# Adaptive-norm modulation blocks as fp32 column-group products in a two-layer hybrid backbone

## The chip, the cores and the metric

One NeuronCore of one Trainium2 chip runs the whole program in one launch. The metric is the device time of a run in microseconds (us). The engines are PE (TensorE: matmuls, with its weight loads shown apart as PEld), DVE (VectorE), ACT (ScalarE), POOL (GpSimd) and SP (SyncE, which here only issues transfers). They run side by side, and each works through its own instructions in order.

## The reference

Two layers work on 256 latent and 256 context tokens of width 1024. Each layer is a SwiGLU feed-forward (FFN) half-step, a token mixer, and a second FFN half-step. Every sub-layer is modulated by columns that come from one product per layer, of a conditioning vector with a 1024 x 9216 matrix:

```python
m_lat = (silu(c) @ w_ada[l] + b_ada[l])       # 9 * 1024 columns, for the latent tokens
m_ctx = silu(c_ctx) @ w_ada[l] + b_ada[l]     # the same matrix, for the context tokens

def modulate(xs, m, j):
    return xs * (1 + m[3 * j + 1]) + m[3 * j]

def ffn_sublayer(xs, m, j, wg, wu, wd, g, b):
    y = 0.5 * swiglu(modulate(xs, m, j), wg, wu, wd)
    return layer_norm(ALPHA * xs + m[3 * j + 2] * y, g, b)
```

## The kernel before, in words

Activations lie transposed: 8 chunks of 128 features (`k` or `j`) by 512 token columns (context first, then latent). Each fp32 operand of a large product is split into a high and a low part (`whi`/`wlo` for a weight, `hH`/`hL` for the modulated input, `aH`/`aL` for the FFN's inner activations), and PE runs three products of the parts (line 420, 256 columns each). ACT makes the high part by a cast (line 282), DVE or POOL the low part by a subtraction (`split_lo`, line 620).

The order of all loads is one list, `seq` (lines 169 to 205): "x" is an input piece, "w" a weight unit of 512 KB, and the rest are pieces of `w_ada`. A block `b` is 512 of the 9216 columns; it comes in four pieces `kp` of 512 KB, each with two of the eight `k`. SP issues the loads in the order of `seq`. Weights and most pieces share five buffers ("raw"); `use_one` (line 271) consumes the next item, and a buffer comes free when its last reader is done. The pieces of blocks 1 and 3 go to the six buffers of another pool (`own_room`).

The modulation blocks are computed in three ways:

- Blocks 0 to 3 of layer 0 ("s" items, lines 291 to 297) hold shift and scale of the first FFN. Each piece is split like a weight on ACT and on DVE or POOL, and `sum_parts` (line 1286) multiplies the parts on PE with the four-column `scol2`; the 4 x 512 rows are copied (`direct_rows`), turned into columns by four transposes (`direct_cols`) and added to the bias (`direct_bias`).
- Most later blocks ("a" items, lines 298 to 322) are summed on DVE: for each `k` and token stream one multiply-add of 128 x 512 (lines 317 and 319), the last one written as halves into a `fold` tile (line 313). `red_step` (line 367), called after each FFN step, then takes the block through four ages: POOL adds the two halves (line 381), ACT and POOL split the sum (lines 385 and 386), PE sums over partitions with `pick` and ACT copies the rows (lines 359 and 364), PE transposes them (line 350) and DVE adds the bias (line 343).
- One block of layer 1 ("p" items, lines 323 to 336) is multiplied directly in fp32, `scol` (two columns) against the raw piece, in the pause of the last mixer's layer norm (`norm_latent`, line 647; `run_direct`, line 410).

At the start (lines 1343 to 1402) PE transposes the inputs (`stream_chunk`), the blocks 0 and 2 give the modulation of chunks 0 to 3, `first_input(j)` (line 1320) builds `hH` and `hL` of chunk j, and `go([j])` (line 439) runs the first four gate and up units (tiles `gu`) over chunk j: 24 products. Blocks 1 and 3 do the same for chunks 4 to 7. `in_turn` (line 1403) later subtracts the token mean, which comes from `xs`, a sum of the chunks on POOL (line 1399), by one PE product (line 1405).

The FFN (`ffn`, line 758) then goes through its gate and up units in steps `m` of 96 products, with the "a" items of layer 0 interleaved, and through the down products (tiles `dn`).

## Time and profile before

| | us |
|---|---|
| median of 3 runs (lowest, highest) | 1822.42 (1820.31, 1823.8) |
| the profiled execution's own time | 1820.95 |
| its span on the core | 1819.2 |

The profile is one execution. Its span is the time from the core's first to its last recorded instruction; the execution's own time is 1.75 us longer, and 1.47 us below the median of the runs. A busy engine is one with an instruction in flight; a matmul's record contains the end of its pipeline, so records of successive matmuls overlap and a steady stream is read from starts per time.

### The profile page before, as it was taken

To read this page: it belongs to the slowest core of one execution; us is meant where nothing else is said; L and a number is where in the kernel's file an instruction comes from. 1 tells how busy PE (TensorE), PEld (TensorE's weight loads), DVE (VectorE), ACT (ScalarE), POOL (GpSimd) and SP (SyncE) were. 2 spreads that over 40 slices of the span, in tenths; PEclk is the share of its full clock that TensorE was granted. 3 is DMA by queue.
4 is the path that set the end of the run, shared out by engine and by line. 5 is a ranking of instruction groups with operands and counts; after the bars stand their busy time and mean duration, and the time that the engine had idled before them with its cause. 6 is when DMAs were issued, how large, how long until landed. Compare 5 with 4: busy or idle time off the path is not lost.

```text
span 1819.2 us, 33814 instructions
## 1 busy us (share of the span) xinstructions
PE 1729.1 (95%) x14145; PEld 1658.0 (91%) x14145; DVE 1282.1 (70%) x1857; ACT 742.0 (41%) x1191; POOL 460.2 (25%) x326
## 2 busy tenths in 40 slices
PE   6899999999899999999999999999999989989997
PEld 4789999998798899999999989999999878879997
DVE  6899799956685678866565568865653768676565
ACT  4322232233757545422222364223223466655443
POOL 3435133243542044110101140100000466150000
PEclk8999999999999999999999999999999999999999
DMA  8367555643213225644454326665563232357662
GB/s 292 98 187 204 151 171 169 185 126 93 71 47 93 70 71 147 185 140 143 127 172 120 90 59 185 178 183 159 179 184 95 82 105 70 105 158 214 183 198 83
DMA packets 375080, 253.32 MB, mean 139 GB/s; under 512 B 8144, under 2 KB 336336, under 8 KB 374928
## 3 DMA queue, kind: packets, MB, share of 16 engines
q1 hardware_dynamic: 373856, 248.81, 46.4%
q8 instruction: 111, 1.82, 0.4%
q0 software_dynamic: 1072, 2.36, 0.4%
q14 instruction: 41, 0.34, 0.1%
HBM read 250.09 MB, written 1.05 MB: 138 GB/s over the span
## 4 chain that ended last, share of the span: by engine, by line
PE 74%; DVE 17%; ACT 5%; issue 2%; DMA 1%; POOL 0%; SPq 0%; DVEq 0%; ACTq 0%
PE gu L420 39%; PE dn L420 21%; PE head L420 5%; DVE acc L319 3%; PE pj L420 3%; PE wo L420 2%; DVE wlo L620 1%; DVE ri L939 1%; DVE h L1324 1%; PE o L1133 1%; DVE aL L620 1%; DVE xl L906 1%; ACT whi L282 1%; DVE xT L754 1%; PE adap L359 1%
## 5 line engine op out<-in xcount | busy, mean ns | idle before, releaser
L420 PE MATMUL gu<-hH,whi 128*128 128x256 f32 x2336 | 493.8, 281 | 8.3 <-ACT hH L1326 6.8
L420 PE MATMUL gu<-hH,wlo 128*128 128x256 f32 x2336 | 492.2, 280 | 6.8 <-DVE wlo L620 6.4
L420 PE MATMUL gu<-hL,whi 128*128 128x256 f32 x2336 | 492.2, 280 | 1.7 <-POOL hL L620 0.9
L282 ACT CAST whi<-raw 128x1024 fp32r<-128x1024 f32 (+1 forms) x319 | 318.8, 1025 | 177.6 <-PE dn L420 70.8
L420 PEld LDWEIGHTS gu<-hH,whi 128*128 128x128 f32 x2336 | 372.0, 190 | 13.0 <-ACT hH L1326 7.3
L420 PEld LDWEIGHTS gu<-hH,wlo 128*128 128x128 f32 x2336 | 371.9, 190 | 7.8 <-DVE wlo L620 7.2
L620 DVE TENSOR_TENSOR wlo<-raw,whi 128x1024 fp32r<-128x1024 f32 (+2 forms) x250 | 313.2, 1256 | 88.0 <-ACT whi L282 79.9
L420 PEld LDWEIGHTS gu<-hL,whi 128*128 128x128 f32 x2336 | 370.7, 190 | 2.5 <-DVE hL L620 1.4
L620 POOL TENSOR_TENSOR wlo<-raw,whi 128x1024 fp32r<-128x1024 f32 (+2 forms) x110 | 217.0, 1979 | 440.2 <-ACT whi L282 414.8
L319 DVE SCALAR_TENSOR_TENSOR acc<-raw,scol,acc 128x512 f32<-128x512 f32 x337 | 291.4, 912 | 1.0
L420 PE MATMUL dn<-aH,whi 128*128 128x256 f32 x1280 | 285.0, 282 | 6.0 <-DVE xT L754 2.9
L420 PE MATMUL dn<-aL,whi 128*128 128x256 f32 x1280 | 280.7, 279 | 0.3 <-DVE aL L620 0.3
L420 PE MATMUL dn<-aH,wlo 128*128 128x256 f32 x1280 | 280.8, 279 | 0.0
L420 PEld LDWEIGHTS dn<-aH,whi 128*128 128x128 f32 x1280 | 208.4, 189 | 11.1 <-DVE xT L754 4.5
L420 PEld LDWEIGHTS dn<-aH,wlo 128*128 128x128 f32 x1280 | 208.0, 189 | 0.2
L420 PEld LDWEIGHTS dn<-aL,whi 128*128 128x128 f32 x1280 | 207.4, 188 | 0.7 <-DVE aL L620 0.7
L767 ACT CAST aH<-pr 128x512 fp32r<-128x512 f32 (+1 forms) x88 | 50.0, 568 | 369.0 <-DVE pr L766 369.0
L766 DVE TENSOR_TENSOR pr<-sg,gu 128x512 f32<-128x512 f32 (+1 forms) x84 | 51.6, 614 | 166.0 <-PE gu L420 111.1
L754 DVE SCALAR_TENSOR_TENSOR xT<-dn,gate,xT 128x256 f32<-128x256 f32 x174 | 78.0, 478 | 83.5 <-PE dn L420 83.0
L381 POOL TENSOR_TENSOR fold<-fold 128x512 f32<-128x512 f32 x24 | 49.3, 2054 | 267.1 <-DVE fold L313 267.1
L420 PE MATMUL pj<-hH,whi 128*128 128x256 f32 x384 | 84.7, 289 | 5.3 <-ACT pt L1102 2.8
L364 ACT COPY rows<-adap 2x512 f32<-2x512 f32 x31 | 17.5, 575 | 162.2 <-PE adap L359 162.2
(267 smaller groups left out, 2377.4 us busy)
## 6 DMA issues: line engine op xcount, KB each, us to landing
raw<-in_w_ada_dram SPq DMA_DIRECT2D x136, 512.0 KB, 4.6
raw<-in_ff_gate_dram SPq DMA_DIRECT2D x88, 512.0 KB, 4.1
raw<-in_ff_up_dram SPq DMA_DIRECT2D x88, 512.0 KB, 4.7
raw<-in_ff_down_dram SPq DMA_DIRECT2D x64, 448.0 KB, 4.0
raw<-in_w_in_dram SPq DMA_DIRECT2D x36, 512.0 KB, 3.9
raw<-in_ff_down_dram SPq DMA_DIRECT2D x32, 512.0 KB, 4.4
raw<-in_w_out_dram SPq DMA_DIRECT2D x16, 512.0 KB, 3.6
in<-in_w_ada_dram SPq DMA_DIRECT2D x8, 512.0 KB, 6.7
```

Source lines behind the costliest of these rows:

```text
L282: S.copy(h_[:, :n], t[:, :n])
L319: V.scalar_tensor_tensor(out=a[:, st], in0=t[:, kk * 512:(kk + 1) * 512], scalar=sc_, in1=a[:, st], op0=ALU.mult, op1=ALU.add)
L359: PE.matmul(pp[0:2, :], lhsT=pick[:, n - 1], rhs=parts[:, i], start=(i == 0), stop=(i == 1))
L381: G.tensor_tensor(out=a[:, 0], in0=a[:, 0], in1=a[:, 1], op=ALU.add)
L420: PE.matmul(o[:, c], lhsT=w, rhs=X[:, k, c], start=first and i == 0, stop=last and i == len(halves) - 1)
L620: (eng or V).tensor_tensor(out=dst_l, in0=src, in1=dst_h.bitcast(F32), op=ALU.subtract)
L754: V.scalar_tensor_tensor(out=xT[:, j, a:b], in0=ps[:, a:b], scalar=gate[:, st, j:j + 1], in1=xT[:, j, a:b], op0=ALU.mult, op1=ALU.add)
L766: V.tensor_tensor(out=pr[:, c], in0=sg[:, c], in1=up[:, c], op=ALU.mult)
L767: S.copy(aH[:, m, c], pr[:, c])
L906: V.scalar_tensor_tensor(out=t3[:, :, off:], in0=s3[:, :, :256 - off], scalar=w[tp], in1=t3[:, :, off:], op0=ALU.mult, op1=ALU.add)
L939: V.reciprocal(gates[c, d][0], gates[c, d][0])
L1133: PE.matmul(o[c][r, a:b], lhsT=vk[c][:, x_ * 128 + 64 * p_:x_ * 128 + 64 * p_ + 64], rhs=pt[c, p_, h][:, kc * 256:(kc + 1) * 256], start=( ...
```

## The change

Blocks 0 to 3 of layer 0 become "p" items: no split, but the raw piece is multiplied in fp32. The stationary operand is `scol_z`, 32 columns per `k` of which two are `scol` and 30 zero; it lies in the tile `AB`, which the mixer overwrites, so `padded_scol` writes it at the start and again in `run_direct`. Product `k` writes the 32 PSUM partitions of column group `k % 4`. `to_cols` multiplies the copied 128 x 512 result with `join`, which adds the four groups while it turns rows into columns. The token mean comes from eight fp32 products on PE between blocks 0 and 2, in place of POOL's sum. Later blocks lose two ages: DVE adds the halves, and `to_cols` with an fp32 `pick` takes the place of split, sum, copy and transposes. `first_input` writes `hH` from `xT` on ACT. In `norm_streams` the reductions of the last two blocks are gone, since `red_step` no longer keeps any.

```diff
-    pick = const.tile([128, 2, 2], F32R, name="pick")
+    pick = const.tile([128, 2, 2], F32, name="pick")
+    join = const.tile([128, 2], F32, name="join")
+    scol_z = AB[:, 0].rearrange("p a (k s) -> p (a k) s", s=32)
...
-    seq = [("x", i) for i in range(4)] + [("s", 0, b, kp) for b in (0, 2) for kp in range(4)]
-    seq += [("w", u) for u in range(4)] + [("s", 0, b, kp) for b in (1, 3) for kp in range(4)]
+    seq = [("x", i) for i in range(4)] + [("p", 0, b, kp) for b in (0, 2) for kp in range(4)]
+    seq += [("w", u) for u in range(4)] + [("p", 0, b, kp) for b in (1, 3) for kp in range(4)]
...
-        elif it[0] == "s":
-            h_, l_ = part_tiles(*it[2:])
-            n = 512 if it[2] > 1 and it[3] == 3 else 1024
-            for a in range(0, 1024, n):
-                S.copy(h_[:, a:a + n], t[:, a:a + n])
-                split_lo(l_[:, a:a + n], t[:, a:a + n], h_[:, a:a + n], eng)
-            parts.append((it, h_, l_))
...
-                PE.matmul(acc[l, b][0:2, :], lhsT=scol[:, k, :], rhs=t[:, kk * 512:(kk + 1) * 512],
-                          start=(k == 0), stop=(k == KD - 1))
+                PE.matmul(acc[l, b][32 * (k % 4):32 * (k % 4) + 32, :], lhsT=scol_z[:, k, :],
+                          rhs=t[:, kk * 512:(kk + 1) * 512], start=(k < 4), stop=(k >= 4))
...
+    def to_cols(a, w, pool=None):
+        tp = (pool or mps)("adat")
+        for q in range(4):
+            PE.matmul(tp[:, q * 2:q * 2 + 2], lhsT=a[:, q * 128:(q + 1) * 128], rhs=w, start=True, stop=True)
+        return tp
+
+    def direct_rows(l, b):
+        r = s512("rows")
+        S.copy(r, acc.pop((l, b)))
+        return r
...
             if age == 1:
                 a = acc.pop((l, b))
-                if needs_ctx(l, b):
-                    G.tensor_tensor(out=a[:, 0], in0=a[:, 0], in1=a[:, 1], op=ALU.add)
+                if n == 2:
+                    V.tensor_tensor(out=a[:, 0], in0=a[:, 0], in1=a[:, 1], op=ALU.add)
                 r[3] = a[:, 0]
             elif age == 2:
-                part = acc_p.tile([128, 2, 512], F32R, tag="acc", name="part")
-                S.copy(part[:, 0], r[3])
-                split_lo(part[:, 1], r[3], part[:, 0], G)
-                r[3] = part
-            elif age == 3:
-                if len(pend_red) <= keep:
-                    continue
-                red_sum(r)
-                red_rows(r)
-            elif age == 4:
-                ada_finish(l, b, r[3])
+                ada_bias(l, b, to_cols(r[3], pick[:, n - 1]), 2)
                 pend_red.remove(r)
...
+    def padded_scol():
+        G.memset(scol_z, 0.0)
+        V.tensor_copy(scol_z[:, :, 0:2], scol)
+
     def run_direct():
+        padded_scol()
         while seq[ptr["use"]][0] == "p":
             use_one()
...
-            S.copy(hH[:, j], h32)
+                by = [mod[:, i, st, j:j + 1] for i in range(2)]
+                S.activation(out=hH[:, j, a:b], in_=xT[:, j, a:b], func=AF.Identity, scale=by[0], bias=by[1])
...
+        use(4)
+        rows = [direct_rows(0, 0)]
+        mp = mps("mean")
+        for j in range(KD):
+            PE.matmul(mp, lhsT=onesD, rhs=xT[:, j], start=(j == 0), stop=(j == KD - 1))
+        mean = s512("xmean")
+        S.activation(out=mean, in_=mp, func=AF.Copy, scale=ALPHA)
+        use(4)
+        direct_bias(0, rows[0])
+        rows.append(direct_rows(0, 2))
+        direct_bias(2, rows[1])
+        for j in range(4):
+            use(1)
+            first_input(j)
         tl = [gps("gu") for _ in range(4)]
         go = proj_start(list(range(4)), tl, (hH, hL), True)
-        go([0], 0, 512)
...
+        for j in range(4):
+            go([j], 0, 512)
+            use((0, 2, 2, 4)[j])
+        rows = [direct_rows(0, b) for b in (1, 3)]
+        for b, r in zip((1, 3), rows):
+            direct_bias(b, r)
-        xs = s512("xs")
-        for j in range(1, KD):
-            G.tensor_tensor(out=xs, in0=xs if j > 1 else xT[:, 0], in1=xT[:, j], op=ALU.add)
         for j in range(4, 8):
             first_input(j)
```

On PE, between the input transposes and the first `gu` products (`adap` are the modulation products, `adat` the turning of rows into columns, `mean` the token mean), before:

```order
L1333 MATMUL xtp<-cs,in 128x128 x32
L1293 MATMUL adap<-whi,scol_146 4x512 x2
L1293 MATMUL adap<-wlo,scol_146 4x512 x2
...
L1310 MATMUL adat<-cs,rows 128x4 x4
L1293 MATMUL adap<-whi,scol_146 4x512 x2
L1293 MATMUL adap<-wlo,scol_146 4x512 x2
L1310 MATMUL adat<-cs,rows 128x4 x4
L420 MATMUL gu<-hH,whi 128x256 x2
```

and in the change:

```order
L1271 MATMUL xtp<-cs,in 128x128 x32
L315 MATMUL adap<-raw,AB 32x512 x8
L1288 MATMUL mean<-xT,onesD 128x512 x8
L315 MATMUL adap<-raw,AB 32x512 x8
L332 MATMUL adat<-join,rows 128x2 x8
L391 MATMUL gu<-hH,whi 128x256 x2
```

Thirty-two products on split parts became sixteen on the raw pieces, with the eight mean products between the two blocks and both turnings behind the second block.

On DVE, at the same place (`h` is the modulated chunk in fp32, `hL` its low part, `wlo` the low part of a weight), the change has:

```order
L1275 COPY xT<-xtp 128x512 x4
L1254 TENSOR_TENSOR mod<-adat,add_152 128x2x4 x2
L591 TENSOR_TENSOR wlo<-raw,whi 128x1024
L1263 TENSOR_SCALAR h_286<-xT,mod 128x256 x2
L591 TENSOR_TENSOR hL<-h_286,hH 128x512
L591 TENSOR_TENSOR wlo<-raw,whi 128x1024
L1263 TENSOR_SCALAR h_298<-xT,mod 128x256 x2
```

The splits of the `w_ada` pieces are gone from it, and the low parts of the four weights, two of them POOL's before, now alternate with the chunks.

On PE, in the layer norm of the last mixer (`wo` is the output projection's last product, `m` the norm's sums), before:

```order
L420 MATMUL wo<-aL,whi 128x256
L329 MATMUL adap<-raw,scol 2x512 x2
L497 MATMUL m_17990<-s_17782,onesD 128x256
L497 MATMUL m_17991<-s_17783,onesD 128x256
L329 MATMUL adap<-raw,scol 2x512 x6
L420 MATMUL gu<-hH,whi 128x256
```

and on DVE in the change, where the copy into `AB` stands behind the norm's last step (`L494` and `L497` normalise chunk 0):

```order
L490 TENSOR_TENSOR m_17658<-y,m_17658 128x256
L494 TENSOR_TENSOR xT<-xT,y 128x256
L378 COPY AB<-scol 128x8x2
L497 TENSOR_TENSOR xT<-xT,m_17658 128x256
```

PE keeps its order there, but the six products now read `AB`, and so come after this copy.

## Rows read from the trace of the kernel before

**Rows 1.** The page, part 1: busy time, share of the span, instructions by engine.

```profile
PE 1729.1 (95%) x14145; PEld 1658.0 (91%) x14145; DVE 1282.1 (70%) x1857; ACT 742.0 (41%) x1191; POOL 460.2 (25%) x326
```

**Rows 2.** Windows: stretch, length, busy us (matmuls started) per engine, granted clock, DMA.

```profile
80.00:180.00 100.00, 90.97 (x744) 88.62 (x743) 97.23 (x117) 29.07 (x40) 42.67 (x27) 0.97 0.60 180
240.00:260.00 20.00, 20.00 (x179) 20.00 (x178) 19.58 (x29) 6.16 (x8) 8.28 (x4) 1.00 0.53 155
280.00:320.00 40.00, 38.23 (x317) 36.23 (x316) 39.69 (x58) 11.84 (x16) 16.34 (x8) 1.00 0.62 184
```

**Rows 3.** Waits of PE from 72 to 190 us: total, times, longest.

```profile
PE gu L420 <- DVE wlo L620: 5.9, 3, 2.5
PE dn L420 <- ACT aH L767: 2.8, 1, 2.8
```

**Rows 4.** Timeline of PE at the start: start us, length us, instruction, [idle before <- releaser].

```profile
10.20 6.06 PE L1333 MATMUL xtp<-cs,in 128*128 128x128 f32 x29 [0.78 <-DMA in<-in_x_dram]
...
32.17 0.80 PE L420 MATMUL gu<-hH,whi 128*128 128x256 f32 x2 [4.08 <-ACT hH L1326]
...
61.57 0.50 PE L420 MATMUL gu<-hH,whi 128*128 128x256 f32 x2 [0.99 <-ACT hH L1326]
...
75.00 1.02 PE L1405 MATMUL mean<-xs,onesD 128*128 128x512 f32 x2
```

**Rows 5.** The page, part 6: loads, KB each, median us from issue to landing.

```profile
raw<-in_ff_gate_dram SPq DMA_DIRECT2D x88, 512.0 KB, 4.1
```

**Rows 6.** Timeline of DVE, at the start and in the FFN.

```profile
26.90 1.23 DVE L620 TENSOR_TENSOR wlo<-raw,whi 128x1024 fp32r<-128x1024 f32 x1 [0.70 <-ACT whi L282]
...
28.70 2.77 DVE L1324 TENSOR_SCALAR h<-xT,mod 128x256 f32<-128x256 f32 x2
...
65.88 0.69 DVE L620 TENSOR_TENSOR hL<-h,hH 128x512 fp32r<-128x512 f32 x1 [0.69 <-ACT hH L1326]
66.49 0.74 DVE L1324 TENSOR_SCALAR h<-xT,mod 128x256 f32<-128x256 f32 x2
...
129.63 2.73 DVE L319 SCALAR_TENSOR_TENSOR acc<-raw,scol,acc 128x512 f32<-128x512 f32 x4
```

**Rows 7.** Timeline of ACT: a copy of rows, and a high part straight from `xT`.

```profile
24.36 0.57 ACT L1304 COPY rows<-adap 4x512 f32<-4x512 f32 x1
...
1620.78 0.60 ACT L634 ACTIVATE hH<-xT,mod 128x256 fp32r<-128x256 f32 x1 [0.87 <-DVE xT L526]
```

**Rows 8.** Timeline of PE in the first mixer: turnings, and products on two column halves.

```profile
560.82 0.60 PE L1092 MATMUL vtp<-cs,vt 128*128 128x128 f32 x4
...
561.82 2.81 PE L1133 MATMUL o<-pt,vtok 128*64 128x256 f32 x24
```

**Rows 9.** Groups by line, PE, whole run: count | busy us, mean ns | idle before.

```profile
L359 PE MATMUL adap<-part,pick 128*2 128x512 f32 x62 | 19.2, 399 | 0.0
...
L350 PE MATMUL adat<-cs,rows 2*128 2x2 f32 x128 | 12.5, 201 | 0.0
```

**Rows 10.** Groups by line, POOL, 72 to 190 us.

```profile
L620 POOL TENSOR_TENSOR wlo<-raw,whi 128x1024 fp32r<-128x1024 f32 x10 | 28.3, 2827 | 69.2 <-ACT whi L282 69.2
L381 POOL TENSOR_TENSOR fold<-fold 128x512 f32<-128x512 f32 x4 | 6.8, 1694 | 3.6 <-DVE fold L313 3.6
L620 POOL TENSOR_TENSOR part<-fold,part 128x512 fp32r<-128x512 f32 x4 | 6.3, 1567 | 0.4 <-ACT part L385 0.4
```

**Rows 11.** Groups by line, DVE, 72 to 190 us.

```profile
L319 DVE SCALAR_TENSOR_TENSOR acc<-raw,scol,acc 128x512 f32<-128x512 f32 x60 | 62.1, 1091 | 0.0
L620 DVE TENSOR_TENSOR wlo<-raw,whi 128x1024 fp32r<-128x1024 f32 x10 | 14.4, 1438 | 0.3 <-ACT whi L282 0.3
```

**Rows 12.** Timeline of PE in the last mixer's layer norm.

```profile
1609.68 3.55 PE L329 MATMUL adap<-raw,scol 128*2 128x512 f32 x4 [2.05 <-DVE xT L754]
...
1614.63 5.31 PE L329 MATMUL adap<-raw,scol 128*2 128x512 f32 x12
1621.43 0.38 PE L420 MATMUL gu<-hH,whi 128*128 128x256 f32 x1 [1.49 <-ACT hH L634]
```

More of the change, by code (lines that the diff above doesn't have):

```diff
@@ L211 @@
     acc = {}
-    parts = []
     pend_red = []
@@ L700, in norm_streams @@
         advance(head[2], G)
-        for r in pend_red:
-            assert r[2] == 3
-            red_sum(r, gps)
+        assert not pend_red
         for i, _ in enumerate(nm.newton(cc)):
@@ L825, in ffn @@
                 proj([u], [t], (aH, aL), c0, c1)
-                red_step(2 if last and nxt else 0)
+                red_step()
                 add_gated(j, t, gate, sts)
@@ L1403, in in_turn @@
         def in_turn():
-            mp = mps("mean")
-            PE.matmul(mp, lhsT=onesD, rhs=xs, start=True, stop=True)
-            mean = s512("xmean")
-            S.activation(out=mean, in_=mp, func=AF.Copy, scale=ALPHA)
-            yield
             for j in range(KD):
```

141 lines of the change are left out of this document (21 added, 120 removed).

## The prediction

> **What bounds the kernel now.** I read the busy shares first: PE is busy 95% of the span, so the time is PE's work plus the places where PE starves [rows 1]. Then the windows, to find those places. Well fed, PE starts 179 products in 20 us, 0.112 us each [rows 2]. From 80 to 180 us it starts 744 where 895 would fit; the 151 missing are worth 16.9 us. DVE is busy 97 of these 100 us, and the granted clock is 0.97: part of the stretch ran at the lower of its two levels, 1.2 instead of 2.4 GHz, which comes after PE's pauses. From 280 to 320 us the same is seen in small: 317 of 358, 4.6 us [rows 2]. The waits name the releasers, low weight parts and high parts of activations, both due behind DVE's queue, 8.7 us in all [rows 3]. Last I followed the first 76 us in order of time. The input transposes end at 16.3 us. The first gate product starts at 32.2, the products of chunk 4 at 61.6, and the first step's last product is followed by the mean, over at about 75.9 with two records of 0.43 us [rows 4]. This first step holds 192 products, 21 us of work; the rest of its 43 us is waiting for modulation blocks and for DVE.
>
> So the change touches a bound in two places: the start, where everything waits for blocks 0 to 3, and the stretch up to 180 us, where DVE sets the pace.
>
> **Prices.** One fp32 product over 512 columns shows as two records, which start 0.43 us apart, 0.855 in all (the mean: 1.02 minus the last record's 0.59 is 0.43) [rows 4]. What four column groups make of it no row shows. The nearest are the mixer's products on two halves of the columns: 24 records over 256 columns in 2.81 us, 0.11 us each after the tail, where one such record alone would take 0.214 [rows 8]. The two halves ran side by side in full. The lower bound is four side by side, 0.214 us per product of 512 columns; the upper bound is none, 0.855. I take 0.214, since the row is at its own full factor.
> The Trainium skill states another rule ("TensorE: Matmul & The Clock Gate", Part 3, The mechanism): matmuls start and end in strict program order, whatever their place in the array. This case's two-group row does not decide it for four groups. It is the second case below.
>
> **The start, part by part.** Removed are 16 splits (each 1.05 us on ACT and 1.2 on DVE or 2.4 on POOL), 64 short products (0.31 us of busy time each by the nearest form [rows 9]) and POOL's seven sums. Added are 32 fp32 products, eight for the mean, and the copies of 128 rows, which I price as the copies of four rows were, 0.57 us [rows 7], ACT's time going by columns.
>
> - The transposes end at 16.3 as now; four pieces have landed by then or soon after. Block 0: 8 x 0.214 = 1.7, to 18.0. The mean: 8 x 0.855 = 6.8, to 24.8; it stands ahead of block 2, so block 2 pays for it although its pieces, issued as block 0 frees the buffers and 4.1 us in flight [rows 5], land by 23. Block 2: to 26.5.
> - Copy 0.6, four turnings of two records each at 0.11 (four records in 0.60 with a tail of 0.27 [rows 8]), 0.9, and the bias, 0.2: 28.2. ACT writes the two halves of `hH` in 1.1 [rows 7]. First gate product at 29.4, 2.8 earlier than now.
> - From there DVE sets the pace: per chunk one low weight part 1.23, `h` 0.74, `hL` 0.69 = 2.66 [rows 6]. `h` costs 0.74 and not the 2.77 of now, because POOL has no work there. Chunk 0 needs the fourth weight: 3 x 2.66 + 1.23 = 9.2, to 37.5. The second weight's load waits for block 2's first piece (25.3), lands at 29.4, and is just in time.
> - PE has had little to do by then, so I let chunk 1 begin at the low clock: 1.7 lost. Three chunks of 24 products, 8.1, and blocks 1 and 3, 3.4: 50.7. The last copy, two turnings, the bias and `hH`, partly overlapped: 3.7. Chunk 4 at 54.4, against 61.6.
> - Chunks 4 to 7 are 96 products, 10.7, with `hH` and `hL` (1.4 per chunk) ahead of PE's 2.7; with 0.6 for the first low part PE is free at 65.7, against 75.9: **-10**. Bounds: -12 if the clock stays up, +11 if no groups overlap.
>
> **The DVE-bound stretch.** The next step's weights and sums on DVE begin as much earlier, so the gain stays. There POOL's work slows DVE: four multiply-adds take 2.73 us undisturbed, 0.68 each [rows 6], but 60 of them took 62.1; with the low parts at 1.44 instead of 1.23 DVE lost 62.1 - 41 + 2.1 = 23 us [rows 11] to POOL's 41.4 [rows 10], 0.56 per us. The four folds and four splits that leave POOL are 13.1 us and give back 7.4. The added sums on DVE, four at 0.69 as `hL` of the same size [rows 6], take 2.8: -4.6. Shorter pauses should leave the clock up, worth at most 0.03 x 100 = 3 us [rows 2]; I take -2.4. Together **-7**. Bounds: +3 (POOL's work cost DVE nothing, the sums remain) and -12.9, which is all that PE misses there, 16.9 less some 1 us for each of four blocks' own products.
> From 280 to 320 us, by the same reasons and up to 4.6 us: **-1**.
>
> **Later blocks on PE.** A block now costs two products and four transposes, 0.62 + 0.40 of busy time [rows 9]. It will cost eight records at 0.11 (as the turnings [rows 8]), or 0.07, the spacing of the two-row transposes (four in 0.40 with a tail of 0.2), and one tail: 0.75 to 1.07. Thirty times -0.27 to +0.05 is -8 to +2. I take the upper price, since the stationary tile has 128 rows, less a little for the fewer starts: **-1**. The casts and row copies that leave ACT (two per block), and POOL's work past 320 us, cost nothing now: PE is fed there. They gain nothing either. The two ages less mean that PE waits for DVE's sum one step earlier; it is queued a step ahead of that, just behind a low part that PE needs anyway, so nothing new is late.
>
> **The last norm.** The direct block ran in PE's pause, its last six products from 1614.6 to 1619.9 [rows 12]. They now read `AB`, which DVE writes one operation ahead of the chunk that ACT reads at 1620.8 [rows 7], so at about 1620.4. Twelve records at the low clock, 0.85 each in four groups, take 2.6 plus a tail: the next product starts at 1624 instead of 1621.4. These records then stand where the first products did their slow ones (after a pause four records took 3.55 us, with none twelve took 5.31 [rows 12]), so I let a good half come back: **+1**. Bounds: 0, and +5 for two groups at the low clock. POOL's clearing of `AB` is done long before, behind four low parts.
>
> **The sum** is -10 - 7 - 1 - 1 + 1 = -18, made against the profiled execution's 1820.95: 1803. The median of the runs is 1.5 above that execution, so I forecast **1804**.
>
> **The rivals.**
>
> - *Two in flight.* If the second record of a product must start before the first of the next group, a product takes 0.43 us: 32 x 0.214 = 6.8 more at the start and about 1 at the last norm, **1812**. The two-group row cannot exclude it. By the Trainium skill's rule of strict order ("TensorE: Matmul & The Clock Gate", Part 3), this is how it would go.
> - *The DVE stretch gives nothing.* The sums added to DVE and POOL's remaining low parts keep it the bound, so only the start is gained: **1811**. For it: DVE stays near 97% with or without the folds, and ten of POOL's 18 jobs there remain. Against: 0.56 us lost per us of POOL is the mean over the stretch.
> - *The groups do not overlap*, which is the slower side. Every direct product takes its 0.855 us: 5.1 more each on blocks 0 and 2, 10.3 on blocks 1 and 3, and three at the last norm, 23.5 in all: **1828**. It decides once a product takes more than 0.76 us, where 32 x (0.76 - 0.214) eats up the 18. Against it stands the row with two halves in full overlap; for it, that no 32-column product is in this trace.
> - *All of it.* If the turnings come at the low bound and the pauses vanish, -12 - 10 - 2 - 4 + 0: **1794**.
>
> **Chances.** The forecast 0.55, two in flight 0.23, the idle DVE stretch 0.1, no overlap 0.06, all of it 0.06. The range holds the first three cases with the bounds of the last norm: **1795 to 1816**. A measurement of this kernel can tell about 0.2%, 3.6 us. All but the no-overlap case, and a tail where two cases meet and the loads come late, are faster by more: faster 0.89, same 0.05, slower 0.06.
>
> **What would show each step.** In the profile after: the records of the 32-column products start 0.11 us apart on the mean (0.214 with two in flight, 0.43 with none); the first gate product near 29.4, chunk 4 near 54.4, and PE free for the second step near 66; DVE's multiply-adds nearer 0.85 than 1.09 us from 72 to 190 us; PE starting about 810 products from 80 to 180; the last mixer's next product near 1624 less the gain so far. The forecast is wrong if the products take 0.43 us or more, if loads stall behind the mean (SP holds five buffers until block 2 runs), or if PE still waits over 6 us for low parts in that stretch.

## The result and the profile after

The changed kernel took 1830.77 us in the median of four runs (1828.39 to 1832.03), the kernel before 1821.37 (1819.4 to 1823.8): a ratio of 1.0052 with a 95% interval of 1.0037 to 1.0067, slower by 9.4 us. I had forecast 1804 us, faster with a chance of 0.89, and the range ended at 1816. The profiled execution took 1830.9 us, with a span of 1829.0.

The page's first part, kernel after, answers to [rows 1]: VectorE and GpSimd have lost work as intended, and PE is busy 22 us longer.

```profile
PE 1751.4 (96%) x14241; PEld 1698.2 (93%) x14241; DVE 1224.8 (67%) x1867; ACT 700.6 (38%) x1119; POOL 327.9 (18%) x258
```

The start, timeline of PE, kernel after (start us, length us, instruction, count, [idle before <- releaser]), answers to [rows 4].

```profile
10.26 5.28 PE L1271 MATMUL xtp<-cs,in 128*128 128x128 f32 x29 [0.84 <-DMA in<-in_x_dram]
15.48 1.92 PE L315 MATMUL adap<-raw,AB 128*32 128x512 f32 x16
17.33 7.13 PE L1288 MATMUL mean<-xT,onesD 128*128 128x512 f32 x16
24.40 1.93 PE L315 MATMUL adap<-raw,AB 128*32 128x512 f32 x16
26.25 1.95 PE L332 MATMUL adat<-join,rows 128*128 128x2 f32 x16
...
29.09 0.88 PE L391 MATMUL gu<-hH,whi 128*128 128x256 f32 x2 [0.89 <-ACT hH L1262]
...
50.22 1.92 PE L315 MATMUL adap<-in,AB 128*32 128x512 f32 x16
52.08 1.95 PE L332 MATMUL adat<-join,rows 128*128 128x2 f32 x16
54.91 1.07 PE L391 MATMUL gu<-hH,whi 128*128 128x256 f32 x2 [0.89 <-ACT hH L1262]
```

Up to here nearly all is as forecast: sixteen records of the 32-column products in 1.92 us, the mean 7.1 us, the first gate product at 29.09 (forecast 29.4), chunk 4 at 54.91 (54.4). The waits of PE from 72 to 190 us in the kernel after (us in total, times, longest) answer to [rows 3], 8.7 us:

```profile
PE adat L332 <- DVE fold L356: 0.9, 1, 0.9
PE dn L391 <- DVE xT L718: 0.4, 1, 0.4
```

So the starving stretch is cured too. The loss shows where PE has all it needs. Windows, kernel after: stretch, length, busy us (instructions) of PE, PEld, DVE, ACT, POOL, then granted clock, DMA share, GB/s. The first three answer to [rows 2].

```profile
80.00:180.00 100.00, 98.63 (x818) 98.05 (x817) 95.93 (x131) 24.92 (x30) 30.39 (x19) 0.98 0.65 194
240.00:260.00 20.00, 20.00 (x173) 20.00 (x172) 19.38 (x31) 4.87 (x7) 5.31 (x2) 1.00 0.53 165
280.00:320.00 40.00, 40.00 (x342) 40.00 (x341) 36.73 (x57) 8.21 (x9) 7.89 (x2) 1.00 0.62 184
960.00:1000.00 40.00, 40.00 (x340) 40.00 (x340) 18.96 (x25) 9.93 (x14) 0.00 (x0) 1.00 0.40 114
1700.00:1740.00 40.00, 40.00 (x343) 40.00 (x343) 21.41 (x29) 18.70 (x28) 0.00 (x0) 1.00 0.59 169
```

The last two windows in the kernel before:

```profile
960.00:1000.00 40.00, 40.00 (x342) 40.00 (x341) 21.68 (x26) 10.38 (x14) 5.85 (x2) 1.00 0.47 136
1700.00:1740.00 40.00, 40.00 (x355) 40.00 (x355) 23.44 (x32) 18.72 (x27) 0.00 (x0) 1.00 0.68 193
```

From 80 to 180 us PE starts 818 products instead of 744 (forecast: about 810). But a saturated stretch holds 343 products in 40 us where the kernel before holds 355, at the same clock. The last feed-forward, in which the change touches nothing, ran slower. Before, some saturated stretches are fast (355 in 40 us) and some slow (342); after, all are slow.

In what follows, the **spacing** is the mean distance of successive starts of the split products (`gu`, `dn`, `head`, `pj`, `wo`), taken from the trace's start times over all that lie 105 to 130 ns apart: the unstalled ones at full clock, some 12,900 of 13,200. Before it is 115.5 ns (in half of them 113.3, in most others 117.8), after 118.1. 12,900 times 2.64 ns is 34 us.

### The profile page after: what moved, and what is told of

It reads as the page before. It is cut to its first block, busy times and chain, and to the rows that moved or that the text cites. A ratio compares the mean times of both kernels' runs of the same rounds, so it can differ in the third digit from the quotient of the medians.

```text
span 1829.0 us, 33865 instructions
## 1 busy us (share of the span) xinstructions
PE 1751.4 (96%) x14241; PEld 1698.2 (93%) x14241; DVE 1224.8 (67%) x1867; ACT 700.6 (38%) x1119; POOL 327.9 (18%) x258
## 4 chain that ended last, share of the span: by engine, by line
PE 79%; DVE 15%; ACT 3%; issue 2%; DMA 0%; POOL 0%; SPq 0%; DVEq 0%; ACTq 0%
PE gu L391 42%; PE dn L391 21%; PE head L391 5%; PE pj L391 3%; PE wo L391 2%; DVE acc L304 2%; PE adat L332 1%; DVE ri L903 1%; DVE wlo L591 1%; PE o L1097 1%; DVE xl L870 1%; DVE s L460 1%; DVE xT L718 1%; DVE s L463 1%; PE adap L315 1%
## 5 line engine op out<-in xcount | busy, mean ns | idle before, releaser
L391 PE MATMUL gu<-hH,whi 128*128 128x256 f32 x2336 | 500.1, 283 | 2.0 <-ACT hH L1262 1.8
L391 PE MATMUL gu<-hH,wlo 128*128 128x256 f32 x2336 | 497.4, 282 | 2.1 <-DVE wlo L591 2.1
L391 PE MATMUL gu<-hL,whi 128*128 128x256 f32 x2336 | 497.6, 282 | 1.2 <-DVE hL L591 1.1
L591 POOL TENSOR_TENSOR wlo<-raw,whi 128x1024 fp32r<-128x1024 f32 (+2 forms) x106 | 207.7, 1966 | 1191.3 <-ACT whi L274 1153.7
L591 DVE TENSOR_TENSOR wlo<-raw,whi 128x1024 fp32r<-128x1024 f32 (+1 forms) x245 | 295.5, 1209 | 92.8 <-ACT whi L274 89.5
L304 DVE SCALAR_TENSOR_TENSOR acc<-raw,scol,acc 128x512 f32<-128x512 f32 x337 | 275.2, 864 | 1.0
L729 ACT ACTIVATE sg<-gu 128x512 f32<-128x512 f32 (+1 forms) x84 | 45.3, 539 | 115.5 <-PE gu L391 115.3
L391 PE MATMUL pj<-hH,wlo 128*128 128x256 f32 x384 | 83.1, 285 | 0.0
```

What stands on the lines that cost most here:

```text
L304: V.scalar_tensor_tensor(out=a[:, st], in0=t[:, kk * 512:(kk + 1) * 512], scalar=sc_, in1=a[:, st], op0=ALU.mult, op1=ALU.add)
L391: PE.matmul(o[:, c], lhsT=w, rhs=X[:, k, c], start=first and i == 0, stop=last and i == len(halves) - 1)
L591: (eng or V).tensor_tensor(out=dst_l, in0=src, in1=dst_h.bitcast(F32), op=ALU.subtract)
L729: S.activation(out=sg[:, c], in_=gp[:, c], func=AF.Silu)
```

## The experiments

The one thing in the diff that reaches products it does not change is `join`. It takes a 32-byte slot among the constants, and every tile allocated behind it lies 32 bytes further, the rounded weights `whi` and `wlo` among them; `xT`, `hH`, `hL`, `aH` and `aL` stay. In the built program `hH` starts at byte 32,896 of its partition in both kernels, `whi` at 135,104 before and 135,136 after. The **distance** below is the weights' start minus the activations', modulo 256 bytes: 64 before, 96 after. (All slots and slices of a kind are multiples of 256 bytes apart.) My theory after the result: the distance sets the spacing. The rivals: other engines' traffic takes memory turns from PE, or the added records cost the time. Each ratio in the table is to runs of the kernel before that were made beside that kernel. In *paired slots* the high and the low part of a weight unit are two halves of one tile, 8448 bytes from one pair to the next.

| kernel | distance | spacing, ns | median, us | ratio to before, 95% |
|---|---|---|---|---|
| before | 64 | 115.47 | 1821.37 | |
| after | 96 | 118.11 | 1830.77 | 1.0052 (1.0037 to 1.0067) |
| e1_join_in_slot | 64 | 115.85 | 1808.38 | 0.9931 (0.9908 to 0.9954) |
| e2_join_64 | 128 | 118.67 | 1835.86 | 1.0077 (1.0059 to 1.0096) |
| e3_before_pad32 | 96 | 118.17 | 1848.46 | 1.0147 (1.0127 to 1.0167) |
| e4_join_first | 64 | 115.75 | 1808.40 | 0.9924 (0.9903 to 0.9945) |
| e5_weights_32 | 96 | 118.04 | 1830.61 | 1.0061 (1.0045 to 1.0078) |
| e6_fold_on_gpsimd | 64 | 115.89 | 1808.29 | 0.9931 (0.9909 to 0.9953) |
| e7_pad_early | 64 | 116.25 | 1809.10 | 0.9934 (0.9917 to 0.9952) |
| e9_distance_76 | 76, activations moved | 122.03 | 1878.01 | 1.0321 (1.0304 to 1.0339) |
| e10_before_76 | 76, activations moved | 121.18 | 1883.04 | 1.0358 (1.0340 to 1.0377) |
| e8_76_and_pad | 76, activations moved | 122.20 | 1878.05 | 1.0323 (1.0306 to 1.0341) |
| e11_weights_76 | 76, weights moved | 113.59 | 1790.57 | 0.9833 (0.9818 to 0.9848) |
| e12_weights_88 | 88, weights moved | 114.00 | 1773.00 | 0.9734 (0.9717 to 0.9751) |
| e14_before_88 | 88, paired slots | 114.71 | 1793.75 | 0.9848 (0.9833 to 0.9863) |
| e15_change_88 | 88, paired slots | 116.10 | 1800.70 | 0.9887 (0.9871 to 0.9903) |
| e13_pair_88 | 88, paired slots | 116.58 | 1802.80 | 0.9877 (0.9839 to 0.9915) |
| e16_ring_88_pad | 88, weights moved | 114.11 | 1769.77 | 0.9721 (0.9695 to 0.9746) |

**Undo the shift, and do the shift alone.** Two kernels move nothing but places.

```diff
 # e1_join_in_slot, on the changed kernel
-    pick = const.tile([128, 2, 2], F32, name="pick")
-    join = const.tile([128, 2], F32, name="join")
+    pick_join = const.tile([128, 6], F32, name="pick_join")
+    pick = pick_join[:, 0:4].rearrange("p (a b) -> p a b", a=2)
+    join = pick_join[:, 4:6]
 # e3_before_pad32, on the kernel before, ahead of bmean
+    pad = const.tile([128, 2], F32, name="pad")
```

> The changed kernel with its small weight tile join moved into the unused end of pick's slot, so that every weight, activation and scratch tile lies where it lay before the change. Placement theory (the changed kernel's split products are slower because join pushed the weight tiles 32 bytes on; their mean spacing is 118.1 ns against 115.5 ns before, over some 12,900 unstalled products, 34 us): the spacing comes back to about 115.5 ns, 240 to 260 us holds 177 to 179 product starts instead of 172, and the time is about 1797 us (1790 to 1804). Traffic theory (VectorE and the transfers, no longer held up by GpSimd's folds and less waiting, take SBUF turns from TensorE): nothing moves, 1830 us and 172 starts. Block-cost theory (the eight-record products of the later blocks and the last norm cost the 10 us): nothing moves either, 1830 us.

> The kernel before the change with nothing added but a 32-byte tile at the place of join, written once and never read. Placement theory: its products slow from 115.5 ns to about 118 ns, 240 to 260 us falls from 179 to about 172 starts, and the time rises by about 30 to 34 us, to 1850 to 1856 us. Traffic and block-cost theories: unchanged, 1821 us within 3 us.

Without the shift the change gains 0.7%, 22 us against the kernel after; the shift alone costs the kernel before 1.5%, 26 us against the runs of before beside it. I had expected 1797 and 1850 to 1856: both moved as said, and less far. From e1 to the kernel after, the wider spacing alone would be 29 us (12,900 times 2.26 ns) where the medians differ by 22: in the two traces the intervals outside 105 to 130 ns, which hold the waits, are 5 us shorter in the slower kernel. The last feed-forward of e1 still ran slow. Windows, e1 (columns as above):

```profile
240.00:260.00 20.00, 20.00 (x174) 20.00 (x172) 19.52 (x39) 4.11 (x6) 2.85 (x1) 1.00 0.56 169
280.00:320.00 40.00, 40.00 (x351) 40.00 (x350) 36.55 (x56) 7.76 (x8) 5.37 (x2) 1.00 0.70 202
...
1700.00:1740.00 40.00, 40.00 (x342) 40.00 (x341) 21.93 (x31) 16.98 (x23) 0.00 (x0) 1.00 0.71 200
```

The same windows of e3, in which no instruction of the work differs from the kernel before (179 and 355 there):

```profile
240.00:260.00 20.00, 20.00 (x172) 20.00 (x172) 19.58 (x31) 6.09 (x8) 6.75 (x4) 1.00 0.55 159
...
1700.00:1740.00 40.00, 40.00 (x340) 40.00 (x339) 21.50 (x27) 17.07 (x22) 0.00 (x0) 1.00 0.64 183
```

Traffic and the price of the added records fall as causes of the slower spacing.

**Grid or distance, and whose place.** e2 makes `join` 64 bytes wide; e4 allocates it ahead of `xT`, so that activations and weights move together; e5 puts 32 bytes between the raw and the rounded weights of e1.

```diff
 # e2_join_64, on the changed kernel
-    join = const.tile([128, 2], F32, name="join")
+    join = const.tile([128, 16], F32, name="join")[:, 0:2]
 # e5_weights_32, on e1: pools wraw, gap, whi, wlo in this order
+    gap_p = ctx.enter_context(tc.tile_pool(name="gap", bufs=1))
```

> The changed kernel with join made 64 bytes wide, so that all behind it lies 64 bytes further than before the change instead of 32. Placement theory with a 64-byte grid: as when join is in pick's slot, about 1797 us (1790 to 1804). Placement theory in which the exact places of before matter (or the distance between weights and activations): stays at 1825 to 1835 us. Traffic and block-cost theories: 1830 us.

> The changed kernel with join as the first tile of all, so that the activations move by the same 32 bytes as the weights: the distance between them is that of before the change, and the places themselves are off by 32 bytes. If the place against a 64-byte grid decides: slow as the changed kernel, 1825 to 1840 us (more if the activations' place costs as well), 172 starts or fewer between 240 and 260 us. If the distance between weights and activations decides: about 1797 us, 177 to 179 starts. Traffic and block-cost theories: 1830 us.

> The kernel with join in pick's slot, and a 32-byte tile between the pool of raw weights and that of the rounded weights whi: raw weights and the small constants lie where they lay before, whi and wlo (and the running sums and scratch behind them) 32 bytes further. If the distance between TensorE's two operands (activations and whi, wlo) decides: 172 starts between 240 and 260 us, spacing about 118.1 ns, 1830 us (1826 to 1835). If the raw weights' or the constants' place did it (the cast's and the folds' reads): 1808 us, as with join in the slot.

e4 is as fast as e1 though every place is off by 32 bytes, and e2 is slow on a 64-byte grid: not the grid, but the distance. e5 says that the raw weights and the constants have no part in it. The running sums and the scratch moved with `whi` and `wlo` there; the next experiment has none.

**The products by themselves.** Two probes run split products alone, 96 a group, between the same two activation tiles and weight slices pushed on by some bytes (`hH` on its 64-byte grid, the distance equal to the push).

```python
for k in range(8):
    for w, X in ((whi, hL), (whi, hH), (wlo, hH)):
        for c in (0, 256):
            PE.matmul(o[:, c:c + 256], lhsT=w[:, off + k * 128:off + (k + 1) * 128], rhs=X[:, k, c:c + 256], ...)
```

> Not the backbone: split products alone, 96 a group of the same shape as in the kernel (128x128 weights, 256 columns, fp32r), with the weights' slice pushed on by 0, 32, 64 ... 480, 512, 1024 bytes and by 4, 8 and 16 bytes (groups a to q, r, then s, t, u); once back to back (first letter a), once with two 2-column products between groups (b), once with that and VectorE busy with fold-shaped instructions (c). Group k (320 bytes) has the distance that the kernel before has, counted modulo 512 bytes, l (352) the changed kernel's, m (384) that of join at 64 bytes. Distance theory: spacing depends on the letter in all three passes and does not need VectorE: 113.3 or 117.8 ns for k, 117.5 to 118.7 ns for l, 118.7 ns for m, and 512 and 1024 bytes as 0. If another engine's traffic makes the difference: all groups of a and b near 113.3 ns, and only c slower, by some 4 ns whatever the offset.

> Split products alone again, 96 a group, with the weights' slice pushed on in steps of 4 bytes from 0 to 252 (64 groups, letters aa to hh in base 8), in three passes: a with two 2-column products between groups, b with three 8-column products between them, c with one 32-column product and all of one column half before the other. Distance theory: in pass a 117.8 ns at 64 and 192 bytes, 120 at 0 and 128, 117.3 at 96, 115.7 at 8, as in the coarse probe. If what stands between groups sets the phase in which the two reads run: at 64 and 192 bytes some of the passes show 113.3 ns instead of 117.8 (as stretches of the kernel before do), and at the other distances too the passes differ by 2 ns and more. If only the distance counts, the three passes agree within 0.5 ns at each step.

The table repeats every 256 bytes (first probe, 0 to 224 bytes against 256 to 480), and neither other products between groups nor a busy VectorE changes an entry by more than 0.1 ns in all but a few groups. The largest exceptions are in the last pass of the second probe, which also multiplies one column half before the other: 180 bytes has 118.2, 118.2 and 113.7 ns there, 204 bytes 120.0, 120.0 and 123.1. Some of the table (ns): 0 bytes 119.9, 8 bytes 115.7, 32 bytes 118.3, 96 bytes 117.3 or 118.7, 160 bytes 120.0; and 52, 64, 76 and 88 bytes 113.3 to 113.6 in the second probe. At 64 bytes, the kernel's own distance, the first probe had 117.8 in all three passes and the second 113.5 in all three. Windows of the first probe, one group of 96 at 64 bytes in each (first pass, and last pass with VectorE busy):

```profile
108.30:119.40 11.10, 11.10 (x97) 11.10 (x96) 0.00 (x0) 0.00 (x0) 0.00 (x0) 1.00 0.00 0
...
586.20:597.30 11.10, 11.10 (x96) 11.10 (x96) 10.78 (x10) 0.00 (x0) 0.00 (x0) 1.00 0.01 1
```

And of the second, at 64 bytes and (second row) at 76:

```profile
379.60:390.30 10.70, 10.70 (x97) 10.70 (x95) 0.00 (x0) 0.00 (x0) 0.00 (x0) 1.00 0.01 2
413.20:423.90 10.70, 10.70 (x96) 10.70 (x96) 0.00 (x0) 0.00 (x0) 0.00 (x0) 1.00 0.00 0
```

So the rate depends on how TensorE's two operands lie, with no other engine at work, and at 64 bytes there are two steady rates. Which one a stretch falls into was not set there by what stands just between the groups, since three kinds of it gave one rate; the group that ran ahead differed (32 bytes in the first probe, 60 in the second). That fits the kernel before, whose stretches change between 113.3 and 117.8 ns, but I did not test it further.

**Smaller terms: the folds and the padded copy.** On e1, e6 gives the folds back to GpSimd; e7 writes the padded copy ahead of the last norm, by GpSimd, which also puts the first pair of block 16 behind that copy (in the changed kernel the pair is multiplied ahead of it).

```diff
 # e6_fold_on_gpsimd
-                    V.tensor_tensor(out=a[:, 0], in0=a[:, 0], in1=a[:, 1], op=ALU.add)
+                    G.tensor_tensor(out=a[:, 0], in0=a[:, 0], in1=a[:, 1], op=ALU.add)
 # e7_pad_early: padded_scol() from run_direct to the head of norm_latent
-        V.tensor_copy(scol_z[:, :, 0:2], scol)
+        G.tensor_copy(scol_z[:, :, 0:2], scol)
```

> The kernel with join in pick's slot, with the 24 folds of the two half-height sums given back to GpSimd (as before the change). If the folds on VectorE (24 of 0.68 us) are what eased the stretch from 80 to 180 us by keeping GpSimd off VectorE's reads: VectorE's acc rows slow again, the first feed-forward ends 2 to 5 us later, and the time is 1810 to 1813 us. If GpSimd's split of part, which stays away, was the larger part of the disturbance, or VectorE has room: 1808 us within 1.5 us.

> The kernel with join in pick's slot, with the zero-padded copy of scol for the last blocks written before the last norm begins, and by GpSimd, instead of on VectorE behind the norm's statistics. If that copy holds up the twelve last modulation products (they start at 1599.94 us, 13 us after the last wo product, and the first gate product follows at 1603.50): they start before 1596 us, the span from the last wo product to the first gate product shrinks from 16.7 to about 14 us (14.0 in the kernel before), and the time falls by 2 to 3 us, to about 1805.5 us. If the norm's own chain (the rounding of hH) ends last anyway: the products move and the time stays at 1808 us.

e6 starts the last product of the first feed-forward 2.5 us later (434.57 instead of 432.04) and its multiply-adds take 1.04 us instead of 0.99 from 72 to 190 us. The second is a weak sign: the kernel after, with its folds on VectorE, has 1.04 too, and low parts of 1.22 us against 1.40 in e1 and e6. The total is that of e1; its runs spread over 8 us, so the folds' place is inconclusive below that. In e7 the stretch from the last `wo` product to the first gate product (start to start) is 15.0 us instead of 16.7. GpSimd did the copy behind three low parts, PE waited 6 us for it, and the spacing over the run was 116.25 ns: no gain in total.

**A better distance, first try.** All four activation tiles are cut 20 bytes into one tile, which makes the distance 76.

```diff
 # e9_distance_76 on e1, e10_before_76 on the kernel before
+    acts = const.tile([128, 16392], F32R, name="acts")
+    hH, hL, aH, aL = (acts[:, 5 + 4096 * i:4101 + 4096 * i].rearrange("p (k f) -> p k f", k=8) for i in range(4))
 # e8_76_and_pad on e9, at the end of the second mixer's steps; the copy on GpSimd
+        if not both:
+            padded_scol()
```

> The kernel with join in pick's slot, with the four activation tiles cut out of one tile 20 bytes from its start, so that the distance from activations to weights is 76 bytes modulo 256 instead of 64. The fine probe had 113.4 ns at 76 in all three passes, and at 64 either 113.6 or 117.8 ns from one run to the other. Distance theory: the spacing falls from a mean of 115.85 ns to about 113.4 ns everywhere, 240 to 260 us holds 178 to 179 starts and so does the stretch from 920 to 1040 us (170 a 20 us before), and the time falls by up to 12,900 times 2.4 ns, 31 us, to 1776 to 1785 us. If the phase in which the reads lock also needs luck at 76 bytes: a mixture of 113 and 118 ns, 1790 to 1808 us. If the probe says nothing of the kernel: 1808 us or worse.

> The kernel before the change with its activation tiles moved in the same way, to 76 bytes modulo 256. Distance theory: 12,850 unstalled products go from a mean of 115.47 ns to about 113.4 ns, 27 us, to about 1795 us (1793 to 1800). The change at one and the same distance is then worth the difference between this kernel and the changed one at 76 bytes: my prediction's sum gives 18 us; a theory in which the change as such costs time (block products, last norm) gives zero or less.

> The changed kernel at 76 bytes, and the padded copy of scol for the last blocks written by GpSimd at the end of the second mixer's list of steps, well before the last norm. If that copy alone holds the last products (moved to the norm's start it still made them wait 6 us for GpSimd): the products of the last blocks run between the norm's sums, the span from the last wo product to the first gate product falls from 16.7 to 14 us or less, and the time is 2 to 3 us below that of the changed kernel at 76 bytes. If the norm's own chain ends last: no difference above 1.5 us.

A miss: 121 to 122 ns in the mean, 3.2 and 3.6% slower than before, at a distance for which the probe has 113.3. "Only the distance counts" fell with this. Both operands lie 20 bytes further here than in the next experiment's e11, which has the same distance and 113.6 ns, so the place of the pair costs as well; whether it is the activations' place or the weights', no run separates. Not every such move costs: e4 has both 32 bytes further than e1, at the same spacing. e8 shows its own point: from the last `wo` product to the first gate product 12.3 us, where e9 has 15.8. The total did not fall with it (1878.05 and 1878.01 us).

**Second try: move the weights instead.** The ten weight slots are cut out of one tile, 12 or 24 bytes from its start; activations stay where they were before the change.

```diff
 # e11_weights_76 (3), e12_weights_88 (6), on e1
+    wts = wts_p.tile([128, 10248], F32R, name="wts")
+    wts = [wts[:, 6 + 1024 * i:1030 + 1024 * i] for i in range(10)]
-            h_ = whi_p.tile([128, 1024], F32R, tag="whi", name="whi")
-            l_ = wlo_p.tile([128, 1024], F32R, tag="wlo", name="wlo")
+            slot = next(turn) % 5
+            h_, l_ = wts[slot], wts[slot + 5]
```

In these two, twelve products of an output unit read the weights of the unit that follows in its slot, so they compute something else there; number, shape and place of the products are the same.

> The changed kernel with join in pick's slot, activations back at their place of before, and the ten slots of rounded weights cut out of one tile 12 bytes from its start: distance 76 bytes modulo 256, as in the fine probe, with the activations on their 64-byte grid as there. If the probe's table holds for the kernel when the activations lie as in the probe: 113.4 ns nearly everywhere (178 to 179 starts between 240 and 260 us and a 20 us from 920 to 1040 us), 1776 to 1785 us. If the activations' shift was not what made the earlier trial slow (122 ns at 76 bytes): 120 ns and more again, 1865 to 1880 us. In between (a mixture of 113 and 118 ns): 1790 to 1808 us.

> The same with the weights 24 bytes from the tile's start, a distance of 88 bytes modulo 256; the fine probe had 113.55 ns there. If the table holds: as at 76 bytes, within 3 us, 1776 to 1788 us. If it does not: 117 to 120 ns and 1815 to 1850 us.

The table holds: 113.6 and 114.0 ns, and e12 is 35 us faster than e1. The spacing makes about 24 of these (12,900 times 1.86 ns); in the traces the rest are shorter waits, 6 us of them in the second mixer ahead of the `wo` products. That e11 is 18 us behind e12 at a smaller spacing I can only place in part: 7 us of it arise from the end of the last `head` product to that of the last `wo` product in the second mixer.

**The change at one distance.** Kernel before and changed kernel with the same paired slots at 88 bytes, one scratch tile fewer; e13 adds the early copy.

```diff
 # e14_before_88, e15_change_88 (on e1), e13_pair_88 (with e8's early copy)
+            w_ = wts_p.tile([128, 2112], F32R, tag="wts", name="wts")
+            h_, l_ = w_[:, 6:1030], w_[:, 1030:2054]
```

> The kernel before the change with whi and wlo as the two parts of one tile, cut 24 bytes from its start (stride 8448 bytes, so every slot is 88 bytes from the activations modulo 256), and one scratch tile fewer to make room. Distance theory: the mean spacing falls from 115.47 ns to 113.6 to 114.0 ns (as in the changed kernel at 88 bytes), 19 to 24 us, to 1797 to 1803 us. If the gain at 88 bytes belonged to the changed kernel's order of work: 1815 us or more.

> The changed kernel with join in pick's slot, and the weights as the two parts of one tile at 88 bytes, one scratch tile fewer: the same pools and the same distance as in the kernel before at 88 bytes, so that the difference of the two is the change alone, with the spacing out of play. The prediction's sum says 18 us less than that kernel; the pair at the 32-byte place said 17.7 us, the pair at the old place 14.3 us. If the change as such cost time, it would be no faster than that kernel. About 1780 us (1773 to 1785).

> The same changed kernel at 88 bytes, with the padded copy of scol for the last blocks written by GpSimd at the end of the second mixer's steps. At 76 bytes this shortened the span from the last wo product to the first gate product from 15.8 to 12.2 us, while slower products elsewhere hid it in the total. If that holds with the spacing out of play: 3 to 4 us below the changed kernel at 88 bytes, about 1776 us. If the norm's own chain takes it back: within 1.5 us of it.

This did not take the spacing out of play. e14 runs at 114.7 ns, e15 at 116.1, with 355 products from 1700 to 1740 us in the one and 336 in the other, so the totals cannot be compared as I had meant: e15 is 7 us above e14. Windows, e14 and then e15:

```profile
1700.00:1740.00 40.00, 40.00 (x355) 40.00 (x354) 23.62 (x31) 17.61 (x23) 0.00 (x0) 1.00 0.73 205
```

```profile
1700.00:1740.00 40.00, 40.00 (x336) 40.00 (x335) 22.38 (x30) 16.06 (x21) 0.00 (x0) 1.00 0.68 195
```

e14 is 28 us below the kernel before, of which its spacing makes only 10 (12,900 times 0.76 ns): these slots shorten waits too, and how stays open. e13 has the last norm as said (11.7 us against 14.8) and a spacing still wider, and its median is 2 us above e15. The early copy does shorten the pause, but PE's first products after it come slower (27 in 6 us at a granted clock of 0.60 in e8, 44 at 0.81 in e9): 48 products on, e8 is 1.9 us ahead of e9 where the first gate product was 3.6 ahead, and e13 is level with e15 where it was 3.2 ahead (counted from the last `wo` product). No pair of runs shows the copy in the total.

**The version that the runs point to.** The slots of e12, the early copy of e8, and without the last step of the second mixer's list (`wg`), so that the twelve products come before their slot is written again.

> The changed kernel with the ten weight slots in one tile at 88 bytes (as in e12_weights_88), with the early padded copy by GpSimd, and without the last step of the second mixer's list that prepares one more weight unit: in e12_weights_88 and e11_weights_76 that unit's slot was written ahead of the last twelve products of an output unit, which so read the next unit's weights; here they come behind. If the evenly spaced slots (4096 bytes from one to the next) keep the products at 113 to 114 ns, as they did there, and not in the paired slots (8448 bytes apart, 116.1 and 116.6 ns): 113.5 to 114.2 ns, the last norm 3 us shorter, about 1770 us (1766 to 1776). If the fast stretches of e12_weights_88 were luck in what ran before them: a mixture, 1785 to 1805 us.

1769.77 us, 2.8% under the kernel before (0.9721, interval 0.9695 to 0.9746). Windows, and the last norm in the timeline of PE, e16:

```profile
80.00:180.00 100.00, 98.95 (x854) 98.45 (x853) 96.07 (x138) 24.85 (x30) 26.41 (x19) 1.00 0.66 200
240.00:260.00 20.00, 20.00 (x179) 20.00 (x178) 19.14 (x38) 5.33 (x7) 3.82 (x2) 1.00 0.57 173
...
1700.00:1740.00 40.00, 40.00 (x355) 40.00 (x354) 22.02 (x30) 19.34 (x31) 0.00 (x0) 1.00 0.58 169
```

```profile
1563.17 1.06 PE L318 MATMUL adap<-raw,AB 128*32 128x512 f32 x8
1566.14 1.05 PE L318 MATMUL adap<-raw,AB 128*32 128x512 f32 x4 [1.90 <-DMA raw<-in_w_ada_dram]
1569.63 0.58 PE L393 MATMUL gu<-hH,wts 128*128 128x256 f32 x1 [2.44 <-ACT hH L607]
```

The fast rate holds with e16's order of work as with e12's. Why the paired slots lose it at the same distance stays open.

## Why the prediction was wrong

**The step that failed** is the first: "Well fed, PE starts 179 products in 20 us, 0.112 us each". I took this rate for a constant of the work and gave no term to it. It is a state of the kernel before, not even its only one (342 in 40 us from 960 to 1000 us), and the change moved the weights out of the place where that state occurs. The mean spacing went from 115.5 to 118.1 ns, 34 us over 12,900 products; the 32-byte shift alone cost the kernel before 26 us (e3), and the change without it ran 22 us faster than the change as given (e1). That the shift is the cause is shown; why the distance acts on the rate is not. The diff line to stop at was the one new tile ahead of the pools.

The Trainium skill ("SBUF — State Buffer", Who interferes with whom) gives PE one read port for the moving operand and an independent one for weight loads, and says that PE waits on no one. The probes do not agree with the first: with no other engine at work the spacing goes from 113.3 to over 120 ns with the place of the weights. The second they leave standing as far as VectorE goes: with VectorE busy, the first probe's entries stayed within 0.1 ns of those of the pass before.

**The other terms.** I numbered the split products in order of time and compared their starts, for the two pairs that share a distance and for the change as given (us):

| stretch, by product | forecast | e3 to after (96) | before to e1 (64) | before to after |
|---|---|---|---|---|
| to 193: the start | -10 | -5.3 | -7.7 | -5.5 |
| 193 to 1057: the DVE-bound stretch | -7 | -9.9 | -8.6 | -8.1 |
| 1057 to 3169: rest of the first feed-forward | -1 | 0.0 | -1.6 | +3.1 |
| 3169 to 10225 | -1 | -0.7 | -3.6 | +11.7 |
| 10225 to the last, the last norm in it | +1 | -3.3 | +8.1 | +8.7 |
| sum | -18 | -19.2 | -13.4 | +9.9 |

The last row also holds the last feed-forward with its spacing; the last norm by itself stands below.

At one distance the change is worth -19.2 and -13.4 us on these profiled executions (-17.7 and -14.3 on the medians), and the second has 0.38 ns of wider spacing in it: 12,900 times that is 4.9. With the spacing's part taken out so (a linear estimate, on the profiled spans), four pairs give -18.4 (e3 to after), -18.4 (before to e1), -18.0 (e10 to e9) and -14.5 (e14 to e15). On the medians they are -16.9, -19.2, -15.9 and -11.0, and the pair before to after gives some -24, so the estimate is good to several us and no better. The sum of -18 fits it, and in part by luck: the start gave 5 to 8 us where I had 10, the stretch behind it 8 to 10 where I had 7.

- *Four groups overlap.* 16 records in 1.92 us are 0.11 us each on the mean, the price that I took (in the trace's start times four begin 7 ns apart, and the next four 0.43 to 0.45 us after them); the rival of two in flight (0.214) and that of none (0.43) fall. The strict order of the Trainium skill ("TensorE: Matmul & The Clock Gate", Part 3, The mechanism), as I had read it for the former, costs nothing here.
- *The start, too large by half.* To chunk 4 it is as forecast. Then PE, after 32 short records and a pause of 0.89 us, ran at the lower of its two clock levels: from 55 to 62 us it started 29 products at a granted clock of 0.51, some 31 fewer than at full rate, 3.6 us. I had priced one such spell, at chunk 1. In e1 the spell was shorter (44 products in the same window, granted clock 0.67) and the start worth 7.7. Windows, kernel after:

```profile
55.00:62.00 7.00, 6.75 (x29) 6.25 (x30) 6.30 (x13) 4.24 (x8) 0.00 (x0) 0.51 0.07 23
62.00:70.00 8.00, 8.00 (x70) 8.00 (x69) 4.88 (x8) 1.54 (x2) 1.00 (x1) 1.00 0.67 199
```

- *The stretch to 180 us: nearly right in size, one sign of it wrong.* The multiply-adds did not come "nearer 0.85 than 1.09". Groups of DVE and then of POOL, 72 to 190 us, kernel after (count | busy us, mean ns | idle before), against [rows 10, 11]:

```profile
L304 DVE SCALAR_TENSOR_TENSOR acc<-raw,scol,acc 128x512 f32<-128x512 f32 x60 | 59.4, 1044 | 0.0
...
L591 DVE TENSOR_TENSOR wlo<-raw,whi 128x1024 fp32r<-128x1024 f32 x12 | 14.6, 1218 | 0.1
```

```profile
L591 POOL TENSOR_TENSOR wlo<-raw,whi 128x1024 fp32r<-128x1024 f32 x9 | 26.8, 2974 | 65.2 <-ACT whi L274 65.2
```

  Against the undisturbed 0.68 and 1.23 us VectorE lost 18 us here beside 26.8 us of GpSimd, 0.69 per us and not 0.56 (e1, by the same sum: 17.5 beside 25.2, 0.69). So part of the disturbance that I had laid to the folds and splits seems to have stayed with the low parts. PE's waits for low parts, 5.9 us before, are gone all the same.
- *Later blocks* cost what the upper price said: two-column records start 0.11 us apart, 16 of them in 1.95 us.
- *The last norm* came as forecast, +1. The first gate product follows the last `wo` product by 16.0 us instead of 13.4 (e3 to after), 2.6 later as in the forecast's 1624 against 1621.4, and a good half of that comes back: the 48 products behind the first take 6.73 us instead of 8.46, which leaves 0.9. The copy came 12.3 us after the last `wo` product began, where the forecast's 1620.4 is 13.0 after it. Windows of the 6 us from the first gate product on, e3 and then the kernel after:

```profile
1642.68:1648.68 6.00, 5.08 (x28) 4.88 (x28) 4.61 (x13) 5.84 (x14) 4.66 (x7) 0.72 0.86 205
```

```profile
1626.60:1632.60 6.00, 6.00 (x44) 6.00 (x43) 2.17 (x6) 5.54 (x14) 5.58 (x9) 0.82 0.98 252
```

  Timelines of DVE and of PE, kernel after, the second against [rows 12]:

```profile
1622.83 0.17 DVE L378 COPY AB<-scol 128x16 f32<-128x16 f32 x1
```

```profile
1612.23 1.05 PE L315 MATMUL adap<-raw,AB 128*32 128x512 f32 x4 [1.38 <-DVE xT L718]
...
1623.05 3.63 PE L315 MATMUL adap<-raw,AB 128*32 128x512 f32 x12 [5.81 <-DVE AB L378]
1626.60 0.58 PE L391 MATMUL gu<-hH,whi 128*128 128x256 f32 x1
```

None of the rivals came true: the slower one that I gave (no overlap, 1828) had the time nearly right and the mechanism wrong.

## What to carry to other kernels

A tile of 8 bytes moved all that is allocated behind it by 32 here. Before pricing a change, list which operands of the costliest loop move against each other, and compare the rate of a stretch that the change does not touch: if it differs, the change is measured together with a placement. Measure such a change at both places, and search the place by a probe of the loop alone; here the best place found (e12) lies 35 us below e1, some 24 of it by the spacing, and the change itself is worth 11 to 19 by the estimates above.

## What I had not expected of the hardware

- The rate of fp32r products (128x128 weights, 256 columns) depends on the bytes between their two operands modulo 256, from 113.3 to over 120 ns, and also on where the pair lies: at 76 bytes 113.6 ns in one place and 122 with both operands 20 bytes further.
- At one distance there can be two steady rates, 113.3 and 117.8 ns at 64 bytes, which hold over tens of microseconds; what picks one is open.
- Records with a moving operand of 2 columns (128x128 weights in fp32) start 0.11 us apart: they cost as much as the 32-column products' records over 512 columns, four groups side by side.
